# One trunk layer on one core: a new fixed order for preparation and attention heads, q copies on ScalarE, head 2's query weights made inside head 0

## The chip, the cores and the metric

One of the eight cores of a Trainium2 chip runs the whole program. The metric is device time in microseconds (us) of one execution. The engines of a core are TensorE (PE in the profile, PEld for its weight loads), VectorE (DVE), ScalarE (ACT), GpSimd (POOL) and SyncE (SP, which here only issues transfers).

## The reference

One layer of a diffusion backbone in fp32, D = 1024, 8 heads, for two streams with shared weights: 512 latent tokens and 128 context tokens, 640 columns in all.

```python
mod = silu(cond) @ w_ada + b_ada          # shift1, scale1, gate1, shift2, scale2, gate2
h = rms_norm(x) * (1 + scale1) + shift1
u, q, k, v, gates = split(h @ w_in)
q, k = rope_2d(q), rope_2d(k)             # latent tokens only
s = q @ k.T / 8                           # two maps per head
a = softmax(s0) - lam * softmax(s1)
o = rms_norm(a @ v); y_b = o @ w_proj_b; y_a = pool(u) @ w_proj_a
x += gate1 * ((sigmoid(gA) * y_a + sigmoid(gB) * y_b) @ w_out)
h = rms_norm(x) * (1 + scale2) + shift2
x += gate2 * ((silu(dwconv3(h @ Wa)) * (h @ Wu)) @ w_ffn_out)
```

Latent queries see 128 cached context keys and their own 512; the context tokens see themselves alone. The context's keys and values are outputs too.

## The kernel before

Every matrix product is done in three passes on two halves of each operand: `x = hi + lo`, where hi is x rounded to the reduced format fp32r, and hi*hi + hi*lo + lo*hi are added in PSUM. So each weight (128 x 1024, one 512 KB transfer) costs a cast for hi (ACT, L126) and a subtraction for lo (DVE or POOL, L127) before TensorE can use it; `wcols` and `wload` do this with the engines they are given.

The program has a boot, the attention, a mixing stage, an output stage and a feed-forward stage. The boot makes the modulation vectors and `hT`, the normalised and modulated tokens, transposed, and projects q and k of head 0 and q of head 1 (`q`, `k`, `w` in its list). The order of its steps is written out by hand in the string `BOOT`; each token is a letter for the step and a number: `n` sum of squares (ACT), `i` normalising (DVE), `x` transpose (PE), `y` copy from PSUM (ACT for tiles 0 to 3, DVE for 4), `d`/`l` high and low part of a modulation weight (ACT/DVE), `a` its matmuls, `r` copy of a row (ACT, L418), `c` its turn to columns (PE), `u` putting it away (DVE), `h`, `m`, `t` high part, full and low part of `hT` (ACT, DVE, DVE; the last `t` on POOL), `s`/`z` high and low part of the first q and k weights (ACT/POOL, L447/L451). Every instruction of the list is pinned, that is, it is issued behind all that was written before it for its engine.

The attention goes head by head, by the nine strings of `PHASES`. `Stm` is one score map (token tile t, map m): four matmuls on a PSUM bank of two (`psS`), a row maximum on DVE (`nm`, L688), an exponential on ACT (L690), and with the second map a reciprocal and a product (L695, L696), a scaling (ACT, L697) and the joining of the two maps (DVE, L698). `T` transposes the joined map of the head before, `P` multiplies it by the values. `p` is one of eight steps of a projection of q or k of a coming head, `b` one of twenty of v, and `x` transposes the head's context keys and the cached keys on a bank that it shares with the scores. In these strings only the matmuls are pinned. What the other engines do is put in order by the framework's scheduler.

After a projection `rope` (L555) turns q or k: ACT copies it from PSUM, DVE shuffles it (L561), POOL multiplies by the cosine (L562), DVE by the sine (L563) and adds (L564). `q_part` (L573) then splits q: for each of two halves ACT copies a high part into one half of the partitions of `qd` (L582), DVE makes the low part `ql` (L583), POOL copies the high part into the other half (L584). `k_split` does the same for k: high part by ACT (L598), low part by DVE (L599). `weights` starts the load of a weight and of the next one in a list when the first is used; by it, the first use of v's first weight (`b` in phase 0) starts the load of head 2's q weight, whose low part POOL makes.

Of the kernel before, what the change touches and what calls it, by code (L numbers as in the profile page):

```python
# [14 lines left out]
ALU = mybir.AluOpType  # L15
# [3 lines left out]
P = 128  # L19
D = 1024  # L20
KD = D // P
# [13 lines left out]
COL_U, COL_Q, COL_K, COL_V, COL_G = 0, 512, 1536, 2560, 3584  # L35
# [32 lines left out]
def trunk_kernel(ctx: ExitStack, tc: tile.TileContext, a: dict, o: list):  # L68
    nc = tc.nc
# [7 lines left out]
    w_ada, w_in = a["w_ada"][0], a["w_in"][0]  # L77
# [33 lines left out]
    def f(ap):  # L111
        return ap.bitcast(F32)
# [18 lines left out]
    def wcols(w, c0, ncol, k0, nk, name, eng=nc.vector, cp=nc.scalar):  # L131
        src = w[k0 * P:(k0 + nk) * P, c0:c0 + ncol].rearrange("(k p) n -> p k n", p=P)
        return wload(src, (nk, ncol), name, eng, cp)
# [19 lines left out]
    dve, act, pool = Pin(nc.vector), Pin(nc.scalar), Pin(nc.gpsimd)  # L153
# [138 lines left out]
    with tc.tile_pool(name="boot", bufs=1, reuse_waits="tile") as boot:  # L292
        chunks = [(which, col, q) for q in range(4) for which, col in (("sh1", 0), ("sc1", D))]
        XT_ACT = (0, 1, 2, 3)
        H_POOL = (7,)
        BOOT = ("n0 i0 n1 x0 i1 n2 x1 y0 i2 n3 x2 n4 i3 a00 y1 i4 y2 x3 a01 y3 d10 x4 d11 l10 r0 s0 l11 c0 a10 z0 u0 "
# [4 lines left out]
        pinned[0] = True  # L301
        vc_ = boot.tile([16, P], F32, tag="vc", name="vc")
        vr = boot.tile([V_END - 16, P], F32, tag="vr", name="vr")
# [159 lines left out]
        P0 = {}  # L463
# [20 lines left out]
    PBUFS = 7  # L484
    MIX = "u0 8g n0 1g n1 2g m0 4g n2 u1 1g n3 1g m1 2g n4 1g n5 1g u2 1g m2 2g n6 1g n7 u3 1g m3 14g"
    PHASES = (
# [9 lines left out]
    G, sig = {}, {}  # L496

    def gate_load(j, i):
# [27 lines left out]
    with tc.tile_pool(name="att", bufs=2, reuse_waits="tile") as att:  # L526
# [25 lines left out]
            nc.vector.tensor_tensor(neglam, lsum[:, 1:2], lsum[:, 0:1], ALU.subtract)  # L552
            nc.vector.tensor_scalar(neglam, neglam, LAM_INIT, None, ALU.subtract)

        def rope(ps, name, scale):  # L555

            sh = att.tile([P, TOK], F32, tag="rsh", name=f"rsh_{name}")[:, :LAT]
            y_ = att.tile([P, TOK], F32, tag="ry", name=f"ry_{name}")
            nc.scalar.activation(two(y_), ps[:, :, :HALF], AF.Copy, scale=scale)
            y = y_[:, :LAT]  # L560
            nc.vector.stream_shuffle(sh, y, SHUF)  # L561
            nc.gpsimd.tensor_tensor(y, y, cos, ALU.mult)  # L562
            nc.vector.tensor_tensor(sh, sh, sin, ALU.mult)  # L563
            nc.vector.tensor_tensor(y, y, sh, ALU.add)  # L564
            return y_

        def q_load(h):
            return wcols(w_in, COL_Q + h * P, P, 0, KD, f"q{h}", nc.gpsimd)

        def k_load(h):  # L570
            return wcols(w_in, COL_K + h * P, P, 0, KD, f"k{h}", nc.gpsimd)
# [1 line left out]
        def q_part(h, ps=None, bank=bankP):  # L573
            if ps is None:
                w = weights("q", h)
                ps = bank(f"psq{h}")
                yield from proj_steps(ps, w, hT)
            y = rope(ps, f"q{h}", 0.125)
            qd = [att.tile([P, TOK], F32R, tag=f"qd{m}", name=f"qd{m}_{h}") for m in range(2)]
            ql = QL[h % 2]  # L580
            for (r, o, t), (_, _, l) in zip(MAPS(qd), MAPS(ql)):
                nc.scalar.copy(t[r], y[r])  # L582
                nc.vector.tensor_tensor(l[r], y[r], f(t[r]), ALU.subtract)  # L583
                nc.gpsimd.tensor_copy(t[o], f(t[r]))  # L584
            Q[h] = qd, ql

        def MAPS(pair):
# [37 lines left out]
        def k_part(h, ps=None):  # L625
            if ps is None:
                w = weights("k", h)
                ps = bankP(f"psk{h}")
                yield from proj_steps(ps, w, hT)
            y = rope(ps, f"k{h}", 1.0)  # L630
            k_split(h, y, slice(P, KEYS))
            Y[h] = y

# [88 lines left out]
        def values(h, i):  # L722

            vh, vl = V[h // 2]
            vc = slice((h % 2) * P, (h % 2 + 1) * P)
            if i == 0:
                PO[h] = bank1(f"po{h}")
            po, k0 = PO[h], 2 * i
            pt, th, tl = TT[h, k0]
            for i in range(2):  # L730
                kt = k0 + i
                if kt < 5:
                    mm3(po, vh[kt][:, vc], vl[kt][:, vc], th[:, i, :], tl[:, i, :], kt == 0, kt == 4)
            if k0 < 4:
                return
            pp = pt[:, 1, 256:384]
            mm3(pp, vh[5][:, vc], vl[5][:, vc], th[:, 1, :P], tl[:, 1, :P], True, True)
            nc.scalar.copy(oraw[:, h, :LAT], po)
            nc.scalar.copy(oraw[:, h, LAT:], pp)
            sq = att.tile([P, TOK], F32, tag="rsh", name=f"sq{h}")  # L740
            nc.gpsimd.tensor_tensor(sq, oraw[:, h, :], oraw[:, h, :], ALU.mult)
            sh = att.tile([P, TOK], F32R, tag="th", name=f"sqh{h}")
            sl = att.tile([P, TOK], F32R, tag="tl", name=f"sql{h}")
            nc.scalar.copy(sh, sq)
            nc.vector.tensor_tensor(sl, sq, f(sh), ALU.subtract)
            SQ[h] = sh, sl
# [44 lines left out]
        W = {}  # L791

        def weights(kind, i):

            n = need.index((kind, i))
            for st in need[n:n + 2]:
                if st not in W:
                    W[st] = loads[st[0]](st[1])
            return W[kind, i]

# [14 lines left out]
        def step(h, op):  # L815
            kind, i = op[0], int(op[1:] or 0) if op[0] in "STPm" else 0
            if op[-1] == "g":
                gate_steps(int(op[:-1]))
            elif op[-1] in queue:
                project(op[-1], int(op[:-1] or 1))  # L820
            elif kind == "S":
                attend(h, i // 10, i % 10)
            elif kind == "T":
                turned(h - 1, i)
            elif kind == "P":
                values(h - 1, i)
            elif kind == "m":
                u_pool(i)
            else:
                between(NH + 1 if kind == "z" else h)  # L830
# [175 lines left out]
    h2 = mg  # L1006
# [576 lines left out]
```

## Time and profile before

| | us |
|---|---|
| median of 3 runs | 1090.98 (1090.66 to 1093.48) |
| the profiled execution | 1091.43 |
| its span, first to last instruction | 1089.6 |

The profile is one execution on the hardware. A time of a row is counted from the span's start. Busy time of TensorE is that of its matmuls, whose ends are modelled. The granted clock is given as a share of full speed. In its page TensorE is busy for 1038.0 us of the span, DVE for 851.6, ACT for 543.5 and POOL for 320.8.

### The profile page before, as it was taken

To read this page: it belongs to the slowest core of one execution; us is meant where nothing else is said; L and a number is where in the kernel's file an instruction comes from. 1 tells how busy PE (TensorE), PEld (TensorE's weight loads), DVE (VectorE), ACT (ScalarE), POOL (GpSimd) and SP (SyncE) were. 2 spreads that over 40 slices of the span, in tenths; PEclk is the share of its full clock that TensorE was granted. 3 is DMA by queue.
4 is the path that set the end of the run, shared out by engine and by line. 5 is a ranking of instruction groups with operands and counts; after the bars stand their busy time and mean duration, and the time that the engine had idled before them with its cause. 6 is when DMAs were issued, how large, how long until landed. Compare 5 with 4: busy or idle time off the path is not lost.

```text
span 1089.6 us, 16713 instructions
## 1 busy us (share of the span) xinstructions
PE 1038.0 (95%) x6559; PEld 967.0 (89%) x6559; DVE 851.6 (78%) x1193; ACT 543.5 (50%) x906; POOL 320.8 (29%) x256
## 2 busy tenths in 40 slices
PE   6979999999999999999999999899989999999997
PEld 4778899999999999999998899898779998899986
DVE  5978978988887577776773579998889984699947
ACT  8646666666765552222242465554345542255524
POOL 4544224323222630000000005443374420444202
PEclk9999999999999999999999999999999999999999
DMA  9831212202112135545554022223442322323312
GB/s 312 247 88 51 62 32 69 59 25 71 38 43 59 41 96 157 165 140 159 154 190 141 1 78 59 83 92 93 127 128 82 94 68 68 97 78 94 119 38 97
DMA packets 128481, 106.10 MB, mean 97 GB/s; under 512 B 4174, under 2 KB 110206, under 8 KB 128403
## 3 DMA queue, kind: packets, MB, share of 16 engines
q1 hardware_dynamic: 126450, 101.93, 30.8%
q0 software_dynamic: 1232, 1.80, 0.8%
q8 instruction: 51, 0.84, 0.3%
q10 hardware_dynamic: 720, 1.31, 0.3%
q14 instruction: 28, 0.22, 0.1%
HBM read 101.36 MB, written 3.67 MB: 96 GB/s over the span
## 4 chain that ended last, share of the span: by engine, by line
PE 54%; DVE 28%; ACT 8%; issue 7%; POOL 1%; DMA 1%; SPq 0%; ACTq 0%; DVEq 0%; POOLq 0%
PE ps_g L157 10%; DVE cv L150 7%; PE psyb L157 5%; PE psk L157 3%; PE psu L157 3%; PE psya L157 3%; DVE wlo_f L150 3%; PE s L157 2%; PE acc L157 2%; PE po L157 2%; DVE nm L688 2%; PE psv L157 2%; PE psq L157 2%; ACT cv L150 1%; PE pat L160 1%
## 5 line engine op out<-in xcount | busy, mean ns | idle before, releaser
L150 POOL TENSOR_TENSOR s<-raw_fu 128x512 f32<-128x512 f32 x20 | 33.3, 1666 | 309.1 <-DVE spare L150 155.7
L150 DVE SCALAR_TENSOR_TENSOR cv<-av,vcol,cv 128x511 f32<-128x511 f32 (+1 forms) x80 | 88.8, 1130 | 12.1 <-ACT cv L150 10.8
L157 PE MATMUL ps_g<-hT,whi_g 128*128 128x320 f32 x512 | 96.7, 311 | 0.0
L157 PEld LDWEIGHTS ps_g<-hT,whi_g 128*128 128x128 f32 x512 | 80.2, 188 | 2.0 <-issue 1.5
L690 ACT ACTIVATE p<-s,nm 128x640 f32<-128x640 f32 (+1 forms) x80 | 56.7, 709 | 40.0 <-DVE nm L688 39.4
L688 DVE TENSOR_REDUCE nm<-s 128x1 f32<-128x640 f32 (+1 forms) x80 | 56.5, 709 | 12.4 <-PE s L157 11.0
L157 PE MATMUL psv<-whi_v,hT 128*128 128x256 f32 x320 | 66.0, 286 | 0.0
L157 PE MATMUL ps_g<-hT,wlo_g 128*128 128x320 f32 x256 | 58.3, 309 | 0.0
L150 DVE TENSOR_TENSOR wlo_f<-s,whi_f 128x1024 fp32r<-128x1024 f32 x40 | 51.0, 1298 | 4.7 <-ACT whi_f L150 4.6
L157 PE MATMUL s<-ks,qd 128*128 128x320 f32 x144 | 44.2, 318 | 10.7 <-DVE ks L599 7.1
L157 PEld LDWEIGHTS psv<-whi_v,hT 128*128 128x128 f32 x320 | 53.2, 192 | 0.3 <-ACT whi_v L126 0.3
L157 PE MATMUL psyb<-on,whi_pb 128*128 128x320 f32 x256 | 48.0, 309 | 0.0
L150 ACT CAST whi_f<-s 128x1024 fp32r<-128x1024 f32 x40 | 41.8, 1044 | 12.0 <-POOL s L150 11.9
L157 PE MATMUL psv<-wlo_v,hT 128*128 128x256 f32 x160 | 45.5, 284 | 0.9 <-DVE wlo_v L127 0.9
L157 PE MATMUL s<-ks,ql 128*128 128x320 f32 x144 | 42.9, 308 | 0.0
L157 PEld LDWEIGHTS ps_g<-hT,wlo_g 128*128 128x128 f32 x256 | 42.8, 188 | 0.0
L157 PE MATMUL psk<-hT,whi_k 128*128 128x320 f32 x224 | 42.6, 312 | 0.0
L157 PEld LDWEIGHTS psyb<-on,whi_pb 128*128 128x128 f32 x256 | 40.3, 188 | 0.5
L697 ACT ACTIVATE p<-p,z 128x640 f32<-128x640 f32 (+1 forms) x40 | 29.7, 744 | 20.0 <-DVE z L696 19.8
L157 PEld LDWEIGHTS s<-ks,qd 128*128 128x128 f32 x144 | 27.6, 192 | 13.4 <-POOL ry_q L562 6.8
L698 DVE SCALAR_TENSOR_TENSOR p<-p,z,p 128x640 f32<-128x640 f32 (+1 forms) x40 | 35.0, 878 | 5.4 <-ACT p L697 5.1
L150 POOL TENSOR_TENSOR acc_g<-acc_g,part_g 128x512 f32<-128x512 f32 x16 | 27.9, 1743 | 37.7 <-ACT part_g L150 36.8
(985 smaller groups left out, 3409.9 us busy)
## 6 DMA issues: line engine op xcount, KB each, us to landing
raw_fa<-in_w_ffn_in_dram SPq DMA_DIRECT2D x22, 512.0 KB, 3.8
raw_fu<-in_w_ffn_in_dram SPq DMA_DIRECT2D x22, 512.0 KB, 3.8
raw_fo<-in_w_ffn_out_dram SPq DMA_DIRECT2D x20, 512.0 KB, 3.6
raw_g<-in_w_in_dram SPq DMA_DIRECT2D x16, 512.0 KB, 4.9
raw_g<-in_w_ada_dram SPq DMA_DIRECT2D x16, 512.0 KB, 3.7
araw_sh<-in_w_ada_dram SPq DMA_DIRECT2D x8, 512.0 KB, 7.6
araw_sc<-in_w_ada_dram SPq DMA_DIRECT2D x8, 512.0 KB, 8.3
raw_v<-in_w_in_dram SPq DMA_DIRECT2D x8, 512.0 KB, 6.3
```

The lines of the kernel that those rows point to most:

```text
L150: pin(getattr(self.eng, op)(*args, **kw))
L157: pin(nc.tensor.matmul(out, s, m, start=start, stop=stop, skip_group_check=more))
L160: pin(nc.tensor.transpose(out, x, ident))
L688: nc.vector.tensor_reduce(nm[:, i:i + 1], s, AX.XY, ALU.max, negate=True)
L690: nc.scalar.activation(p.rearrange("p (b n) -> p b n", b=s.shape[1]), s, AF.Exp, bias=nm[:, i:i + 1], accum_out=z[:, i:i + 1])
L697: nc.scalar.activation(p, p, AF.Copy, scale=z[:, 1:2])
L698: nc.vector.scalar_tensor_tensor(A[h, t], A[h, t], z[:, 0:1], p, ALU.mult, ALU.add)
```

## The change

Five things are edited. The string `BOOT` has the same 143 steps in another order. Of the nine phase strings all but that of phase 4 have their steps in another order, and that of phase 0 has one new step, `w`. `rope` takes the engine of the cosine multiply, which is now DVE for q of heads 0 and 1 and for k of head 0, and POOL for the rest. The copy of q's high part into the other partitions is on ACT instead of POOL, in all heads. Head 2's query weight is no longer loaded with the first use of v's weight but at `w` in phase 0, behind the step `x`, with the cast on ACT and the low part on DVE, both pinned there.

```diff
-        BOOT = ("n0 i0 n1 x0 i1 n2 x1 y0 i2 n3 x2 n4 i3 a00 y1 i4 y2 x3 a01 y3 d10 x4 d11 l10 r0 s0 l11 c0 a10 z0 u0 "
-                "y4 v d20 a11 r1 l20 c1 d21 u1 a20 h0 l21 d30 m0 a21 h1 t0 l30 k0 r2 s2 q0 m1 d31 z2 a30 t1 d40 c2 "
-                "l31 k1 d41 l40 q1 a31 l41 d50 w0 r3 l50 c3 d51 w1 u2 u3 l51 h2 a50 a40 h3 m2 a51 t2 d60 a41 m3 r5 "
-                "d61 l60 k2 c5 r4 l61 s1 q2 c4 d70 z1 u5 t3 w2 d71 u4 l70 k3 h4 a60 l71 a70 h5 m4 a61 t4 a71 m5 r6 "
-                "c6 k4 r7 c7 u6 t5 q3 u7 h6 w3 k5 h7 m6 q4 t6 w4 m7 k6 t7 q5 w5 q6 w6 k7 q7 w7 ")
+        BOOT = ("n0 n1 i0 x0 i1 n2 x1 i2 y0 n3 x2 i3 n4 a00 y2 i4 x3 a01 y3 d10 x4 y1 d11 l10 r0 s0 l11 c0 z0 a10 u0 "
+                "y4 v d20 a11 r1 l20 d21 c1 d30 u1 a20 h0 l21 m0 a21 h1 l30 t0 k0 s2 r2 d31 m1 a30 t1 d40 z2 c2 k1 "
+                "l31 q0 d41 l40 a31 l41 d50 w0 q1 r3 c3 l50 d51 w1 u2 u3 l51 h2 a50 h3 m2 a51 m3 a40 t2 d60 a41 r5 "
+                "d61 r4 l60 k2 l61 s1 c4 c5 t3 d70 u5 q2 z1 d71 w2 a60 u4 k3 l70 h4 l71 a70 h5 m4 a61 r6 t4 a71 m5 c6 "
+                "q3 k4 r7 u6 c7 t5 u7 h6 w3 h7 m6 t6 w4 k5 m7 q4 q5 t7 k6 w5 w6 q6 k7 q7 w7")
...
     PHASES = (
-        "3b p 4b 2p 2b S00 S01 2b p S10 2p x p S11 p b S20 2b S21 b S30 3b S31 S40 2b",
-        "3p S00 p S01 2p x 2p T0 S10 4p S11 T1 p P0 p S20 2p S21 P1 T2 2p P2 p S30 p S31 2p S40 2p",
-        "b S00 b S01 b 2p x b T0 b 3p S10 p P0 S11 T1 b p 2b S20 P1 p T2 S21 4b P2 b S30 3b S31 2b S40 2b",
-        "3p S00 S01 2p x T0 3p S10 P0 S11 2p T1 S20 3p T2 p S21 2p P1 P2 S30 3p S31 2p S40 3p",
+        "4b 2p b p 4b S00 b S01 x w b p S10 3p S11 b S20 p 2b S21 3b S30 2b S31 S40 b",
+        "2p S00 2p S01 2p x 2p T0 S10 4p S11 T1 P0 2p S20 2p S21 T2 P1 2p P2 p S30 p S31 2p S40 2p",
+        "b S00 b S01 b 2p b T0 b p x 3p S10 b P0 S11 T1 p 2b S20 P1 p T2 S21 5b S30 P2 3b S31 b S40 3b",
+        "S00 3p S01 2p x T0 3p S10 P0 S11 2p T1 S20 4p T2 p S21 p P1 P2 S30 4p S31 2p S40 2p",
-        "2p S00 S01 2p x T0 4p S10 P0 S11 p T1 2p S20 3p T2 2p S21 P1 P2 p S30 S31 5p S40 2p",
-        "S00 b S01 b p b x 3p S10 p b T0 2p S11 b T1 b S20 p 2b P0 P1 S21 T2 5b S30 b P2 2b S31 b S40 3b",
-        "2p S00 S01 3p x T0 2p S10 p P0 T1 p S11 2p P1 S20 p S21 2p T2 2p S30 P2 p S31 S40 2p",
-        "3p x p m0 m1 p T0 T1 m2 5p T2 P0 p P1 P2 2p 1g m3 3g z 1g")
+        "2p S00 S01 3p x T0 3p S10 P0 S11 p T1 2p S20 3p T2 2p S21 P1 P2 p S30 S31 5p S40 2p",
+        "S00 b S01 b p b x 4p b S10 T0 2p S11 T1 2b S20 p 2b P0 P1 S21 T2 5b S30 b P2 2b S31 b S40 3b",
+        "p S00 p S01 3p x T0 2p S10 p P0 T1 p S11 2p P1 S20 p S21 2p T2 2p S30 P2 p S31 S40 2p",
+        "2p x 2p m0 m1 p T0 T1 m2 5p P0 T2 p P1 P2 2p 1g m3 3g z 1g")
...
-        def rope(ps, name, scale):
+        def rope(ps, name, scale, eng=nc.gpsimd):
-            nc.gpsimd.tensor_tensor(y, y, cos, ALU.mult)
+            eng.tensor_tensor(y, y, cos, ALU.mult)
-        def q_load(h):
-            return wcols(w_in, COL_Q + h * P, P, 0, KD, f"q{h}", nc.gpsimd)
+        def q_load(h, *eng):
+            return wcols(w_in, COL_Q + h * P, P, 0, KD, f"q{h}", *(eng or (nc.gpsimd,)))
...
-            y = rope(ps, f"q{h}", 0.125)
+            y = rope(ps, f"q{h}", 0.125, nc.gpsimd if h > 1 else nc.vector)
             for (r, o, t), (_, _, l) in zip(MAPS(qd), MAPS(ql)):
-                nc.gpsimd.tensor_copy(t[o], f(t[r]))
+                nc.scalar.copy(t[o], f(t[r]))
...
-            y = rope(ps, f"k{h}", 1.0)
+            y = rope(ps, f"k{h}", 1.0, nc.gpsimd if h > 0 else nc.vector)
...
             for st in need[n:n + 2]:
-                if st not in W:
+                if st not in W and (st, kind) != (("q", 2), "v"):
                     W[st] = loads[st[0]](st[1])
...
                 values(h - 1, i)
+            elif kind == "w":
+                W["q", 2] = q_load(2, dve, act)

```

## Rows read from the trace of the kernel before

**Rows 1.** TensorE's waits from 60 to 108.4 us: total, times, longest.

```profile
PE s L157 <- DVE ks L599: 6.6, 1, 6.6
...
PE s L157 <- ACT p L690: 1.7, 2, 1.3
```

**Rows 2.** Windows: stretch, length; busy PE, PEld, DVE, ACT, POOL; clock; DMA share, GB/s.

```profile
60.00:345.00 285.00, 268.27 (x1868) 257.66 (x1867) 238.56 (x384) 187.24 (x364) 88.43 (x67) 0.99 0.18 52
...
75.30:81.90 6.60, 0.03 (x1) 0.01 (x1) 6.34 (x8) 3.53 (x6) 4.20 (x3) 0.74 0.03 8
...
81.90:108.40 26.50, 24.24 (x163) 23.29 (x163) 22.74 (x35) 17.74 (x37) 11.09 (x8) 0.94 0.17 53
```

**Rows 3.** Windows of one microsecond: the first and last of four.

```profile
82.00:83.00 1.00, 1.00 (x4) 1.00 (x5) 0.97 (x2) 0.00 (x0) 0.00 (x0) 0.50 0.00 0
...
85.00:86.00 1.00, 1.00 (x10) 1.00 (x9) 0.85 (x2) 0.82 (x4) 0.00 (x0) 0.87 0.00 0
```

**Rows 4.** Order of time of DVE and POOL, 64 to 83 us: start, duration, instruction.

```profile
66.24 1.23 DVE L127 TENSOR_TENSOR wlo_v<-raw_v,whi_v 128x1024 fp32r<-128x1024 f32 x1 [1.26 <-ACT whi_v L126]
...
67.39 0.74 DVE L561 STREAM_SHUFFLE rsh_q<-ry_q 128x512 f32<-128x512 f32 x1
...
69.45 2.86 POOL L127 TENSOR_TENSOR wlo_q<-raw_q,whi_q 128x1024 fp32r<-128x1024 f32 x1
...
69.97 2.89 DVE L563 TENSOR_TENSOR rsh_k<-rsh_k,sin 128x512 f32<-128x512 f32 x1
...
72.78 1.78 DVE L564 TENSOR_TENSOR ry_q<-ry_q,rsh_q 128x512 f32<-128x512 f32 x1
...
79.28 0.69 DVE L563 TENSOR_TENSOR rsh_q<-rsh_q,sin 128x512 f32<-128x512 f32 x1
...
80.00 2.62 DVE L599 TENSOR_TENSOR ks<-ry_k,ks 64x640 fp32r<-64x640 f32 x2
```

**Rows 5.** Instructions on the tile qd: count, shortest, median and longest ns.

```profile
L582 ACT CAST qd<-ry_q x16: 712/724/731, 74.6 to 288.8; 64x640 fp32r<-64x640 f32 x16
...
L583 DVE TENSOR_TENSOR ql<-ry_q,qd x16: 812/1107/1270, 75.4 to 290.9; 64x640 fp32r<-64x640 f32 x16
```

**Rows 6.** The chain that ended last, 60 to 112 us: start, duration, what.

```profile
92.71 0.87 PE psk L157 x6
...
93.58 0.71 PE psv L157 x6
...
94.30 0.60 PE s L157 x4
```

**Rows 7.** Order of time of POOL, DVE and PE at head 0's end.

```profile
102.67 2.42 POOL L127 TENSOR_TENSOR wlo_q<-raw_q,whi_q 128x1024 fp32r<-128x1024 f32 x1 [3.99 <-ACT whi_q L126]
...
103.25 3.37 DVE L599 TENSOR_TENSOR ks<-ry_k,ks 64x640 fp32r<-64x640 f32 x2
...
106.34 0.31 PE L157 MATMUL s<-ks,qd 128*128 128x320 f32 x1
```

**Rows 8.** TensorE's waits from 108 to 345 us.

```profile
PE mx L160 <- ACT p L690: 3.3, 3, 1.4
...
PE pat L160 <- ACT p L690: 1.5, 1, 1.5
...
PE s L157 <- DVE tl L714: 1.3, 1, 1.3
```

**Rows 9.** Order of time of ACT and PE in the boot.

```profile
13.69 1.91 ACT L382 COPY xT<-pt 128x1024 f32<-128x1024 f32 x2
...
16.29 1.01 ACT L382 COPY xT<-pt 128x1024 f32<-128x1024 f32 x1 [0.69 <-PE pt L160]
...
19.09 0.36 ACT L418 COPY rows_sh<-ps_sh 4x256 f32<-4x256 f32 x1
...
19.50 0.60 PE L157 MATMUL ps_sh<-sel,rows_sh 5*128 5x2 f32 x4 [0.41 <-ACT rows_sh L418]
...
20.86 1.05 ACT L398 CAST xn_sh<-araw_sh 128x1024 fp32r<-128x1024 f32 x1 [0.45 <-DMA araw_sh<-in_w_ada_dram]
```

## The prediction

> **What bounds the kernel now.** I read the page first, then a table of windows over the whole span, then TensorE's waits, and last the order of time where those waits are longest. From 345 us on TensorE is nearly always busy and the change touches nothing there. What can move lies ahead of it. Between 60 and 345 us TensorE is busy for 268.27 of 285 us [rows 2], so 16.7 us are idle. The list of waits says where. One wait alone is 6.6 us: the first score matmul of head 0, held by the DVE operation that makes the low part of head 0's keys [rows 1]. The windows show the same stretch: from 75.3 to 81.9 us TensorE has 0.03 us of work [rows 2]. A second loss hangs on it. After that idle stretch the granted clock stands at 0.50, the lower of its two levels (1.2 instead of 2.4 GHz), for the first scores too, and returns at about 85.9 us [rows 3]; the four windows from 82 to 86 us show 0.50, 0.50, 0.50 and 0.87, which is 1.63 us of work lost. So the hole at head 0 costs 6.6 + 1.6 = 8.2 us. The waits of the later heads are smaller: their three largest groups make 6.1 us together [rows 8]. The largest of them, 3.3 us, is at the step `x`, whose PSUM bank is freed by an exponential on ScalarE.
>
> Why is the hole there? The time order [rows 4] is to be read as two engines in each other's way. DVE shuffles q and k of head 0 from 67.39 us on. Then POOL takes up the low part of head 2's query weights for 2.86 us, and the DVE multiply beside it (128x512, by the sine) takes 2.89 us, where the same operation with POOL idle takes 0.69 us. POOL's cosine multiply of k comes only after that weight, so k is late as well. In the end the low part of k starts at 80.00 us and takes 2.62 us for two.
>
> **The change, part by part.** (1) *The preparation of head 0.* It removes from POOL three cosine multiplies (q0, k0, q1), the weight q2 and the two q copies, and puts the cosines and the weight on DVE, the copies on ScalarE. Without POOL beside them I take 0.69 us for each DVE multiply or add and 0.72 us from start to start [rows 4]. Two shuffles from 67.39 us at a pitch of 0.64 end DVE's first part at 68.67 us. Six operations at 0.72 us (cosine, sine, add for q and for k) end at 73.0 us. ScalarE has four copies for q, the added two priced like the two there now, 0.724 us each [rows 5], so 2.9 us from q's add (70.8) to 73.75 us; then one copy for k to 74.5 us and one DVE subtraction of 0.81 us [rows 5], which gives 75.4 us; the first score needs only this first half of the keys. If the two low parts of q (2 x 0.81) go ahead of k's three operations, it is 76.3 us. The matmuls ahead of the first score are as many as before: 9 `b` and 3 `p` in the old phase string, 9 `b` and 3 `p` in the new one, so the cover still ends at 75.3 us. The wait of 6.6 us becomes 0.1 to 1.0 us; I take 0.6, so 6.0 us saved. With so short a wait the clock has no such idle stretch to fall after, and the 1.6 us come back too: 7.6 us. If POOL's work were gone but DVE did the whole rope of q1 first (a shuffle, three operations and two subtractions, 4.5 us), only about 1.5 us would be saved.
>
> The Trainium skill, page SBUF — State Buffer, section Who interferes with whom, says that a DVE instruction with two SBUF inputs contends with a GpSimd instruction that reads SBUF, and that whoever began first holds the shared port for its whole instruction. The 2.89 us beside 0.69 us [rows 4] agree. By that rule the gain isn't complete, since POOL keeps k1's cosine and the low parts of two weights in head 0, and it speaks for the second case below; the sum would then be the 1088.2 worked out there.
>
> (2) *What DVE has to give back in head 0.* On DVE the change adds 3 x 0.69 us and one weight's low part, 1.23 us like the one of v [rows 4], together 3.3 us. It takes away stretched time: 2.2 us at the sine, 1.1 us at q's add (1.78 against 0.69), 1.0 us at k's low part [rows 4], and in q0 and q1 four times the 0.295 us between median and shortest of that subtraction, 1.2 us [rows 5]: 5.5 us. So DVE ends 2.2 us ahead, no more, if it is what sets the pace up to the first score of head 1, which waits for the low part of k1 that runs 3.37 us for two beside POOL's 2.42 us [rows 7]. Now that score starts at 106.34 us; by DVE alone it would be at 104.1. By TensorE alone: one `p` is 0.87 us, one `b` 0.71 us, one score of four matmuls 0.60 us [rows 6]; from the first score of head 0 at 76 us it has 11 `b`, 7 `p`, eight scores, the shorter last one and the transposes (0.9 us for both, an estimate from the 0.60), 7.8 + 6.1 + 4.8 + 0.9 = 19.6 us, and with 1.5 us of waits for exponentials (1.7 us now [rows 1]) this ends at 97.1 us. One `p` that was ahead of that score before now comes after it, so 0.88 us more work is still to do. The stretch therefore gains between 106.34 - 0.88 - 104.1 = 1.3 us and 106.34 - 0.88 - 97.1 = 8.4 us. DVE is busy 22.74 of the 26.5 us here [rows 2], so it is near the limit but has 3.8 us of gaps to fill, and its low-ranking work (the joining of the two maps) may run after the score. I take two thirds of the added 3.3 us as given back, 2.2 us: 7.6 - 2.2 = 5.4 us gained.
>
> (3) *The later heads.* Between the first score and `x` phase 1 now has 4 `p` for 3, phase 3 has 5 for 2, phase 5 has 3 for 2. At 0.87 us each [rows 6] that is 0.9, 2.6 and 0.9 us more cover, against 3.3 us of waits at three `x` [rows 8]. POOL's q copies no longer stretch q's low part, 0.6 us of DVE a head. Against this ScalarE gets 2 x 0.724 us a head [rows 5], and phase 3 starts its scores without the three `p` ahead. Bounds: 4.6 us saved (the 3.3 us at `x` and the 1.3 us at a score; the 1.5 us at a transpose lie in phase 4, whose string stays), or up to 10.1 us lost (seven heads with 1.45 us each). I take 2.0 us saved: most of the `x` waits go, some of it returns at ScalarE.
>
> (4) *The boot order.* ScalarE's copy of token tile 1 goes behind tile 3 and the first weight cast. ScalarE waits 0.69 us for tile 3 as it is, and without a copy to fill that time the second cast and the copy of the modulation row at 19.09 us come 0.95 us later, half of the 1.91 us that two copies take; TensorE waits for just that row now [rows 9]. Later a DVE low part of h goes behind a weight's, 1.2 us. Against it, ScalarE waits 0.45 us for a transfer soon after [rows 9] and can take that up. Bounds: 1 us gained to 2.2 us lost; I take 0.5 us lost. Head 2's query weight is needed only at the start of phase 1, with 10 `b` and 5 `p` after its step `w` (11.4 us), and this is what hides its cast of 1.05 us (a cast of that size in [rows 9]); its DVE part is priced in (2).
>
> Sum: -5.4 - 2.0 + 0.5 = -6.9 us. The profiled execution took 1091.43 us (span 1089.6), so 1084.5; the median of the three runs lies 0.45 us lower, which gives 1084.0 us.
>
> **The rivals.**
> *DVE sets head 0's pace.* The lower end of (2): only 1.3 us gained there, then -2.0 and +0.5: -2.8 us, 1088.2 us. For it: DVE's 22.74 of 26.5 us. Against: the hole itself comes from an order of work, not from DVE's amount.
> *The later heads lose nearly all waits.* 4.6 us instead of 2.0 in (3), the rest as forecast: 1081.4 us. For it: the extra `p` stand just where the waits are. Against: each head has its own wait, and phases 2 and 4 keep theirs.
> *The wait stays.* DVE's order puts q1's rope or v's low part ahead of k0, 4.5 to 5 us, and the first score comes at 80 to 82 us: 1.0 us saved at the middle, the clock's loss stays, the boot takes its 0.5, nothing else moves, so 1090.5 us. For it: these operations aren't pinned in the text and their order on DVE is the scheduler's. Against: it has placed q0 and k0 first so far [rows 4].
> *Slower: ScalarE's copies delay exponentials.* Two copies stand in ScalarE's queue ahead of an exponential that frees a score bank; if seven heads wait 1.45 us longer for this, 10.1 - 5.4 + 0.5 = +5.2 us, 1096 us. It turns the sign from four heads on (4 x 1.45 = 5.8 us against 4.9). For it: `x` waits for ScalarE already [rows 8]. Against: in 60 to 345 us ScalarE is busy 187.24 of 285 us [rows 2]; the copies bring it to 70%. The Trainium skill, TensorE: Matmul & The Clock Gate, section on the array's architectural detail, calls ScalarE's queue strictly first in, first out; by that rule an exponential can't pass a copy and this case stands at 1096. The trace, where `x` waits for exponentials while ScalarE has idle time elsewhere, doesn't contradict it.
>
> **How the numbers follow.** Chances: forecast 0.50 (its own range 1081.8 to 1086.6), DVE's pace 0.18, later heads 0.17, wait stays 0.08, slower 0.07. The range leaves out the last two and the tail below 1079.5: 1079.5 to 1089.0. About 0.3%, 3.3 us, is what a measurement here tells from no change: the line is 1087.7. Faster are forecast, later heads and 0.07 of DVE's pace, 0.74; within the bound 0.11 and the 0.08, 0.19; slower 0.07.
>
> **What would show it.** Right: no idle stretch over 1 us before head 0's first score and that score at about 76 us, a granted clock of 1.00 throughout 70 to 90 us, the sine multiplies of q0 and k0 at 0.7 us each, and head 1's first score at about 100 us. (2) is wrong if that score waits for k1's low part by more than 4 us. (3) shows in TensorE's waits at `x`: 3.3 us now, under 1.5 then. (4) shows in TensorE's wait for the modulation row, 0.41 us now [rows 9]. The whole is wrong if the first score still waits for DVE, or if ScalarE's exponentials become what most scores wait for.

## The result, and the profile after

The changed kernel takes 1081.38 us in the median (1080.8 to 1083.6, six runs), the kernel before on the same chip 1093.37 us (1090.66 to 1095.63, six runs). The ratio is 0.9896, with a 95% interval of 0.9877 to 0.9915. The profiled executions have spans of 1079.8 and 1089.6 us, 9.8 us apart. (The medians are 12 us apart: the kernel before was profiled in one of its shorter executions.)

First TensorE's waits after the change, as total, times and longest: the first two lines are of 60 to 100 us, the third of 100 to 345 us.

```profile
PE s L157 <- ACT p L690: 2.7, 3, 1.4
...
PE s L157 <- ACT qd L584: 0.3, 1, 0.3
...
PE pat L160 <- ACT p L690: 3.3, 2, 1.8
```

The wait of 6.6 us for the keys' low part in [rows 1] is gone; in its place the first score waits 0.3 us for a copy on ScalarE (L584). No wait at `x` is left of the 3.3 us in [rows 8], but 3.3 us stand at transposes (`pat`), where there were 1.5.

Windows after (stretch, length; busy PE, PEld, DVE, ACT, POOL; clock; DMA share, GB/s):

```profile
60.00:345.00 285.00, 276.09 (x1934) 265.65 (x1933) 239.24 (x410) 202.78 (x387) 69.48 (x55) 1.00 0.18 54
70.00:80.00 10.00, 9.41 (x69) 8.74 (x68) 9.11 (x15) 6.89 (x13) 0.20 (x1) 1.00 0.11 32
80.00:90.00 10.00, 9.68 (x69) 9.22 (x68) 8.91 (x17) 9.20 (x16) 1.08 (x2) 1.00 0.25 74
```

In the same 285 us TensorE is busy 276.09 us where it was 268.27 [rows 2], and the granted clock is 1.00 from 70 to 90 us, where it had fallen to 0.50 [rows 3]. ScalarE is at 202.78 of 285 us, 71%.

The order of time after, from the preparation of head 0 to head 1's first score (start, duration, instruction, idle time ahead of it):

```profile
69.09 0.67 DVE L562 TENSOR_TENSOR ry_q<-ry_q,cos 128x512 f32<-128x512 f32 x1
69.68 0.68 DVE L563 TENSOR_TENSOR rsh_q<-rsh_q,sin 128x512 f32<-128x512 f32 x1
...
71.49 0.68 DVE L564 TENSOR_TENSOR ry_q<-ry_q,rsh_q 128x512 f32<-128x512 f32 x1
...
73.01 1.67 DVE L583 TENSOR_TENSOR ql<-ry_q,qd 64x640 fp32r<-64x640 f32 x2 [0.24 <-ACT qd L582]
...
73.75 1.48 ACT L598 CAST ks<-ry_k 64x640 fp32r<-64x640 f32 x2
...
74.71 1.67 DVE L599 TENSOR_TENSOR ks<-ry_k,ks 64x640 fp32r<-64x640 f32 x2
75.25 1.48 ACT L584 CAST qd<-qd 64x640 fp32r<-64x640 f32 x2
76.03 0.41 PE L157 MATMUL s<-ks,qd 128*128 128x320 f32 x1 [0.27 <-ACT qd L584]
...
83.27 1.22 DVE L150 TENSOR_TENSOR wlo_q<-raw_q,whi_q 128x1024 fp32r<-128x1024 f32 x1
...
89.28 2.40 POOL L127 TENSOR_TENSOR wlo_k<-raw_k,whi_k 128x1024 fp32r<-128x1024 f32 x1 [8.92 <-ACT whi_k L126]
...
94.26 2.35 POOL L127 TENSOR_TENSOR wlo_q<-raw_q,whi_q 128x1024 fp32r<-128x1024 f32 x1 [0.88 <-ACT whi_q L126]
...
94.78 0.67 DVE L662 TENSOR_TENSOR v<-psv,v 128x512 fp32r<-128x512 f32 x1
...
95.82 0.33 PE L157 MATMUL s<-ks,qd 128*128 128x128 f32 x1 [1.43 <-ACT p L690]
...
98.98 1.67 DVE L599 TENSOR_TENSOR ks<-ry_k,ks 64x640 fp32r<-64x640 f32 x2
99.95 0.39 PE L157 MATMUL s<-ks,qd 128*128 128x320 f32 x1 [0.93 <-ACT p L690]
```

The cosine and sine multiplies of q0 take 0.67 and 0.68 us on DVE, one behind the other, where a sine beside POOL had taken 2.89 us [rows 4]. Both halves of k0's low part take 1.67 us (2.62 before [rows 4]), those of k1's 1.67 us too (3.37 before [rows 7]). Head 2's query weight has its low part at 83.27 us in 1.22 us, six microseconds ahead of POOL's next weight. Head 1's first score is at 99.95 us instead of 106.34 [rows 7].

To see where the 9.8 us came from, four moments of each trace are enough. A is the first matmul of v on the low part of the second half of its weight, just behind the end of the boot's work on TensorE. B is the first score of head 0, C its last (the 128x128 form), D the first matmul of the mixing stage (`psu`). The column D-A leaves out the boot. D is read to 0.1 us, and what is worked out from it is good to about that. One thing in it is not equal work: the new string of phase 0 has 19 `b` ahead of C, the old one 18, so with a new string B to C holds 0.71 us more [rows 6] and C to D as much less.

| kernel | A | B-A | C-B | D-C | D-A | span |
|---|---|---|---|---|---|---|
| before | 67.52 | 14.40 | 19.79 | 212.2 | 246.4 | 1089.6 |
| changed | 67.94 | 8.09 | 19.79 | 209.1 | 237.0 | 1079.8 |
| e1_q2_back | 69.44 | 10.24 | 22.01 | 209.7 | 242.0 | 1087.8 |
| e2_cos_pool | 69.64 | 8.90 | 21.25 | 210.1 | 240.3 | 1086.7 |
| e3_copy_pool | 68.40 | 8.55 | 25.15 | 210.4 | 244.1 | 1088.7 |
| e4_old_boot | 69.03 | 8.08 | 19.81 | 209.1 | 237.0 | 1080.4 |
| e5_old_later | 67.84 | 8.09 | 19.81 | 214.1 | 242.0 | 1086.9 |
| e6_ops_only | 68.90 | 8.09 | 23.41 | 213.7 | 245.2 | 1090.2 |
| e7_order_only | 67.56 | 14.42 | 22.21 | 210.8 | 247.4 | 1091.2 |
| a0_again | 69.82 | 8.08 | 19.83 | 209.1 | 237.0 | 1081.6 |
| v1_low_dve | 68.75 | 8.08 | 20.01 | 207.4 | 235.5 | 1080.1 |
| v2_k1cos_dve | 67.94 | 8.07 | 19.37 | 210.4 | 237.9 | 1081.3 |
| v3_strings | 69.72 | 8.09 | 19.80 | 210.2 | 238.1 | 1082.1 |
| n1_fill | 69.25 | 14.46 | 18.87 | 216.4 | 249.8 | 1095.8 |

Before against changed: +0.4 to A, -6.3 to B, 0.0 to C, -3.1 to D. From D to the end it is 775.7 and 774.9 us, -0.8. Together -9.8.

### The profile page after: what moved, and what is told of

It is laid out like the page before. It is cut to its first block, busy times and chain, and to the rows that moved or that the text cites. A ratio compares the mean times of both kernels' runs of the same rounds, so it can differ in the third digit from the quotient of the medians.

```text
span 1079.8 us, 16691 instructions
## 1 busy us (share of the span) xinstructions
PE 1036.0 (96%) x6559; PEld 966.0 (89%) x6559; DVE 844.0 (78%) x1197; ACT 554.3 (51%) x922; POOL 294.2 (27%) x236
## 3 DMA queue, kind: packets, MB, share of 16 engines
q10 hardware_dynamic: 720, 1.31, 0.3%
## 4 chain that ended last, share of the span: by engine, by line
PE 53%; DVE 25%; ACT 9%; issue 8%; POOL 2%; DMA 1%; SPq 1%; ACTq 0%; DVEq 0%; POOLq 0%
PE ps_g L157 10%; DVE cv L150 7%; PE psyb L157 5%; PE psk L157 3%; DVE wlo_f L150 3%; PE psu L157 3%; PE psya L157 3%; PE s L157 2%; PE psv L157 2%; PE acc L157 2%; PE po L157 2%; PE psq L157 2%; DVE nm L688 1%; ACT cv L150 1%; DVE acc_g L150 1%
## 5 line engine op out<-in xcount | busy, mean ns | idle before, releaser
L126 ACT CAST whi_g<-raw_g 128x1024 fp32r<-128x1024 f32 x16 | 16.8, 1049 | 43.1 <-PE ps_g L157 23.7
L157 PE MATMUL pb<-mg,whi_f 128*128 128x320 f32 x176 | 38.7, 307 | 0.0
```

The costliest lines, as they stand in the source:

```text
L126: cp.copy(hi[:, :n], rv)
L157: pin(nc.tensor.matmul(out, s, m, start=start, stop=stop, skip_group_check=more))
```

## The experiments

Ratios are against the kernel before on the same chip, with 95% intervals. The first four each undo one part of the change.

**e1_q2_back**: head 2's query weight is again started by v's first weight, with POOL for its low part.

```diff
-                if st not in W and (st, kind) != (("q", 2), "v"):
+                if st not in W:
-        "4b 2p b p 4b S00 b S01 x w b p S10 3p S11 b S20 ...
+        "4b 2p b p 4b S00 b S01 x b p S10 3p S11 b S20 ...
```

> The changed kernel with head 2's query weight back where it was: loaded with the first use of v's weight, its low part on POOL. Theory (POOL and DVE block each other when both read SBUF, so POOL's 2.9 us stretch a DVE operation of head 0's keys by up to 2.2 us): head 0's first score waits 1.5 to 2.5 us instead of 0.3 and the span is 0.5 to 2.5 us over the changed kernel's 1079.8 us. Rival (the harm before was POOL's queue alone, with k's cosine behind the weight; the cosine is on DVE now): that score stays at 76.0 us within 0.3, and the span stays or falls by up to 1 us, since DVE is rid of 1.2 us in head 0.

Measured: 0.9951 [0.9932, 0.9969], 1088.48 us. D-A is 242.0 against 237.0, so the weight's place and its engine together are worth 5.0 us; no run moves one of the two alone. Order of time, and a window of two microseconds behind the first score:

```profile
70.46 2.41 POOL L127 TENSOR_TENSOR wlo_q<-raw_q,whi_q 128x1024 fp32r<-128x1024 f32 x1 [8.26 <-ACT whi_q L126]
70.59 2.83 DVE L562 TENSOR_TENSOR ry_q<-ry_q,cos 128x512 f32<-128x512 f32 x1
...
79.68 0.41 PE L157 MATMUL s<-ks,qd 128*128 128x320 f32 x1 [2.43 <-ACT qd L584]
```

```profile
81.00:83.00 2.00, 2.00 (x10) 1.96 (x9) 1.85 (x4) 1.34 (x3) 0.00 (x0) 0.50 0.00 0
```

The collision of [rows 4] is back, with the multiply by the cosine in the sine's place: 2.83 us beside POOL's 2.41. The first score then waits 2.43 us, as forecast, and the clock falls to 0.50 behind it. The cost is double the upper end of the forecast: 2.1 us are lost ahead of the first score, 2.2 more up to C and 0.7 behind it. The Trainium skill, SBUF — State Buffer, section Who interferes with whom, has DVE instructions with two SBUF inputs wait while GpSimd holds their common port; these rows agree.

**e2_cos_pool**: the three cosine multiplies back on POOL.

```diff
-            y = rope(ps, f"q{h}", 0.125, nc.gpsimd if h > 1 else nc.vector)
+            y = rope(ps, f"q{h}", 0.125, nc.gpsimd)
-            y = rope(ps, f"k{h}", 1.0, nc.gpsimd if h > 0 else nc.vector)
+            y = rope(ps, f"k{h}", 1.0, nc.gpsimd)
```

> The changed kernel with the cosine multiplies of q0, k0 and q1 back on POOL. Theory (an operation on POOL holds up DVE's one beside it, so nothing is gained by two engines): POOL needs about 1.3 us where DVE needs 0.7, the sines beside it stretch, head 0's first score comes 1 to 2 us later than 76.0, span +0.5 to +2. Rival (they overlap, so DVE is spared 0.7 us for each): the first score comes 0 to 1 us earlier, span -1 to 0.

Measured: 0.9936 [0.9916, 0.9955], 1086.34 us; D-A 240.3, so 3.3 us for this part. The order of time on the two engines:

```profile
70.32 1.31 POOL L562 TENSOR_TENSOR ry_q<-ry_q,cos 128x512 f32<-128x512 f32 x1 [7.91 <-DVE rsh_q L561]
70.80 1.38 DVE L563 TENSOR_TENSOR rsh_q<-rsh_q,sin 128x512 f32<-128x512 f32 x1
71.57 1.76 POOL L562 TENSOR_TENSOR ry_k<-ry_k,cos 128x512 f32<-128x512 f32 x1
72.10 1.78 DVE L563 TENSOR_TENSOR rsh_k<-rsh_k,sin 128x512 f32<-128x512 f32 x1
```

A cosine on POOL beside a sine on DVE ends 1.86 us after the first began (70.80 + 1.38 - 70.32) for q, 2.31 us for k. One behind the other on DVE they take 1.27 us (69.09 to 69.68 + 0.68). Here two engines side by side are slower than one. Of the 3.3 us only some 0.8 lie ahead of the first score, less than the 1 to 2 us forecast; 1.5 lie between B and C, where `x` waits 1.6 us for an exponential, and 1.1 behind C. So the whole cost is above the forecast.

**e3_copy_pool**: the second copies of q's high part back on POOL, in all heads.

```diff
-                nc.scalar.copy(t[o], f(t[r]))
+                nc.gpsimd.tensor_copy(t[o], f(t[r]))
```

> The changed kernel with the copies of q's high part back on POOL in all heads. Theory (the copies stretch DVE's low part beside them, 0.3 us each): span +1 to +3 us. Rival (ScalarE is what the scores wait for in the changed kernel: 6.6 us of TensorE's waits between 60 and 345 us name its exponentials, and the 16 copies take 11.6 us of its time): these waits shrink by a half or more and the span falls by 1 to 3 us.

Measured: 0.9981 [0.9968, 0.9994], 1091.09 us; D-A 244.1, 7.1 us for this part, more than twice the upper end of the forecast, and 5.4 of them between B and C. The order of time at head 0's end, and a window behind it:

```profile
96.69 2.34 POOL L127 TENSOR_TENSOR wlo_q<-raw_q,whi_q 128x1024 fp32r<-128x1024 f32 x1 [1.73 <-ACT whi_q L126]
96.83 2.74 DVE L564 TENSOR_TENSOR ry_k<-ry_k,rsh_k 128x512 f32<-128x512 f32 x1
...
102.10 0.47 PE L157 MATMUL s<-ks,qd 128*128 128x128 f32 x1 [5.27 <-ACT p L690]
```

```profile
103.00:105.00 2.00, 2.00 (x11) 2.00 (x11) 1.61 (x5) 1.35 (x5) 0.00 (x0) 0.50 0.00 0
```

The low part of a later weight now falls on k1's addition, which takes 2.74 us; the last score of head 0 waits 5.27 us and the clock is at 0.50 behind it. That a relief of ScalarE would make the kernel faster is refuted. How much of the 7.1 us is the copies' own time on POOL and how much is that they push this weight onto the addition isn't told apart.

**e4_old_boot**: the old string `BOOT`, all else as changed.

```diff
-        BOOT = ("n0 n1 i0 x0 i1 n2 x1 i2 y0 ...
+        BOOT = ("n0 i0 n1 x0 i1 n2 x1 y0 i2 ...
```

> The changed kernel with the old order of the boot. Theory (the new boot order costs 0.4 us, as the start of v's second matmuls shows, 67.94 after 67.52 us): span 0.2 to 0.6 us shorter. Rival (the new boot order is part of the gain, because it puts other work beside the first projections): span longer by 0.5 us or more.

Measured: 0.9898 [0.988, 0.9916], 1082.53 us, with D-A of 237.0 as in the changed kernel. The boot's order is worth nothing that can be measured.

The next three split the change into orders and operations.

**e5_old_later**: the old strings of phases 1 to 8; phase 0, boot and engines as changed.

```diff
-        "2p S00 2p S01 2p x 2p T0 S10 4p S11 T1 P0 ...
-        "b S00 b S01 b 2p b T0 b p x 3p S10 ...
...
+        "3p S00 p S01 2p x 2p T0 S10 4p S11 T1 p P0 ...
+        "b S00 b S01 b 2p x b T0 b 3p S10 ...
...
```

> The changed kernel with the old strings from phase 1 on; boot, phase 0 and the engines stay as changed. From the start of v's second matmuls to the first matmul of the pooling projection the kernel before takes 246.4 us, the changed one 237.0. Theory (of these 9.4 us, 3.5 us fall after head 0's end, and the new strings bring them by putting cover before x): 239 to 241 us, the waits at x back at 2 to 3.3 us. Rival (they come from POOL's relief, the strings bring nothing): 236.5 to 238 us.

Measured: 0.9958 [0.9944, 0.9973], 1088.95 us; D-A 242.0, so the later strings are worth 5.0 us with the new engines, 1.0 us more than the upper end of the forecast. An order of time around TensorE's largest single wait from 110 to 345 us, three windows of this phase 2, and the cast of the same phase in the kernel before:

```profile
140.07 1.09 PE L160 MATMUL pat<-ident,p 128*128 128x128 f32 x8
...
142.78 1.48 ACT L584 CAST qd<-qd 64x640 fp32r<-64x640 f32 x2
144.16 1.00 ACT L713 CAST th<-pat 128x1024 fp32r<-128x1024 f32 x1
...
146.48 0.41 PE L157 MATMUL s<-ks,qd 128*128 128x320 f32 x1 [1.96 <-DVE tl L714]
```

```profile
146.00:148.00 2.00, 1.52 (x9) 1.52 (x10) 1.83 (x4) 0.00 (x0) 0.00 (x0) 0.87 0.00 0
148.00:150.00 2.00, 2.00 (x7) 1.71 (x7) 0.20 (x1) 1.29 (x3) 0.00 (x0) 0.50 0.00 0
150.00:152.00 2.00, 2.00 (x11) 1.76 (x11) 0.65 (x2) 0.00 (x0) 0.00 (x0) 0.77 0.13 38
```

```profile
148.64 1.02 ACT L713 CAST th<-pat 128x1024 fp32r<-128x1024 f32 x1
```

This is the place where ScalarE's new copies cost something. The cast `th` of the transposed map (L713) stands behind the two copies of 142.78 us in ScalarE's queue and begins 4.09 us after T0's transposes (140.07 to 144.16); in the kernel before, with the copies on POOL, it was 2.34 us (146.30 to 148.64). `tl` follows on DVE, and the score waits 1.96 us, where the same wait was 1.27 us, the 1.3 of [rows 8]. Then the clock falls: 0.87, 0.50 and 0.77 in three windows of 2 us are 1.7 us lost (0.26 + 1.00 + 0.46). With the 0.7 us of the wait that is 2.4 us. D-C of this kernel is 2.6 us above that of before at equal work (214.1 + 0.71 against 212.2). That the copies are the cause is read from these rows; no run takes them off ScalarE in this order. The new string of phase 2 puts `x` and a `p` between T0 and S10, and the wait is gone. The Trainium skill, TensorE: Matmul & The Clock Gate, section on the array's architectural detail, has ScalarE's queue strictly in order; the row of `th` agrees.

**e6_ops_only**: the old boot and phase strings with the new engines. Since head 2's weight needs a place, `w` is put behind `x`, as in the new string. The edit is shown against the changed kernel.

```diff
-        "4b 2p b p 4b S00 b S01 x w b p S10 3p S11 ...
+        "3b p 4b 2p 2b S00 S01 2b p S10 2p x w p S11 ...
...
```

> The kernel before with the new engines alone: cosines of q0, k0, q1 on DVE, q copies on ScalarE, head 2's query weight at a step w behind x in the old phase 0; boot and phase strings old. Theory (the hole at head 0 is closed by the engines): first score at 76 us, the stretch of 246.4 us falls to 239 to 241.5 us. Rival (the old phase 0 doesn't fit the new engines, so the wait comes back at the next scores): 243 us or more.

Measured: 1.0003 [0.9989, 1.0018], 1092.81 us. The operations alone bring nothing; the rival of the expectation (243 us or more) holds. The hole ahead of B is closed as in the changed kernel (8.09 us), but C-B is 23.41 us. TensorE's waits from 60 to 110 us, the order of time inside head 0, and a window behind C:

```profile
PE s L157 <- ACT p L690: 4.9, 5, 1.9
```

```profile
92.59 2.39 POOL L127 TENSOR_TENSOR wlo_k<-raw_k,whi_k 128x1024 fp32r<-128x1024 f32 x1 [1.13 <-ACT whi_k L126]
93.29 2.78 DVE L150 TENSOR_TENSOR wlo_q<-raw_q,whi_q 128x1024 fp32r<-128x1024 f32 x1
...
99.13 0.41 PE L157 MATMUL s<-ks,qd 128*128 128x320 f32 x1 [1.90 <-ACT p L690]
```

```profile
102.00:104.00 2.00, 2.00 (x12) 2.00 (x11) 2.00 (x4) 1.05 (x3) 1.73 (x1) 0.56 0.00 0
```

Scores wait five times for exponentials, 4.9 us together, and the clock falls behind the last. In this string `x` stands three scores in, so `w` comes ten microseconds later than in the changed kernel, beside POOL's next weight, and its low part takes DVE 2.78 us instead of 1.22. Against e5, which has the new phase 0, D-A is 3.2 us longer (245.2 to 242.0). How much of it is the place of `w`, which was my choice, and how much the order of scores and `p` isn't told apart.

**e7_order_only**: the kernel before with the new strings (without `w`) and its old engines. The edit is shown against the kernel before.

```diff
-        BOOT = ("n0 i0 n1 x0 i1 n2 x1 y0 i2 ...
-        "3b p 4b 2p 2b S00 S01 2b p S10 ...
+        BOOT = ("n0 n1 i0 x0 i1 n2 x1 i2 y0 ...
+        "4b 2p b p 4b S00 b S01 x b p S10 ...
...
```

> The kernel before with the new boot and phase strings alone, no engine moved and no w. Theory: the wait at head 0's first score stays above 5 us and the clock falls after it; only the later heads gain: 243 to 246 us for the stretch that takes 246.4. Rival (the order of the text is what counts): 240 us or less.

Measured: 1.0002 [0.9991, 1.0013], 1094.14 us. The first line is the wait ahead of B, unchanged from [rows 1]; the second shows that head 0 then waits for exponentials too.

```profile
PE s L157 <- DVE ks L599: 6.6, 1, 6.6
PE s L157 <- ACT p L690: 3.3, 2, 3.1
```

D-A makes it a table of four: before 246.4, operations alone 245.2, orders alone 247.4, both 237.0. The orders alone are 1.0 us longer, where the theory had them gain. For the same reason the prices of e1 to e5 are no shares of the gain: 5.0, 3.3, 7.1, 0.0 and 5.0 add up to 20.4 us, and the whole change brings 9.4.

The last five look for the limits of the account.

**a0_again**: the changed kernel once more, beside the variants v1, v3 and n1, with no edit.

> The changed kernel once more, beside the others of this call on one chip: 1081 to 1083 us, stretch from v's second matmuls to the pooling projection 237.0 us.

Measured: 0.9896 [0.9878, 0.9914], 1082.33 us. Its stages repeat to 0.04 us, but A comes 1.9 us later. The windows of 30 to 60 us of the changed kernel's two executions, first and again:

```profile
30.00:60.00 30.00, 29.10 (x209) 24.85 (x208) 27.85 (x40) 19.13 (x30) 13.04 (x13) 0.97 0.83 221
```

```profile
30.00:60.00 30.00, 29.11 (x191) 24.51 (x190) 26.58 (x36) 18.62 (x28) 12.30 (x12) 0.89 0.79 214
```

The same list of instructions was granted 0.97 of the clock once and 0.89 the other time.

**v1_low_dve**: the low parts of the q and k weights on DVE, not POOL.

```diff
-            return wcols(w_in, COL_Q + h * P, P, 0, KD, f"q{h}", *(eng or (nc.gpsimd,)))
+            return wcols(w_in, COL_Q + h * P, P, 0, KD, f"q{h}", *eng)
-            return wcols(w_in, COL_K + h * P, P, 0, KD, f"k{h}", nc.gpsimd)
+            return wcols(w_in, COL_K + h * P, P, 0, KD, f"k{h}")
```

> The changed kernel with the low parts of all q and k weights of heads 2 to 7 on DVE instead of POOL: 1.2 us each on DVE instead of 2.4 us on POOL, 12 of them or so. Theory (a POOL operation that reads SBUF holds up DVE's next one for about as long as DVE would need for the work itself): the stretch of 237.0 us becomes 235 to 238. Rival (POOL's work is mostly hidden, DVE's isn't): 239 us or more.

Measured: 0.9878 [0.9858, 0.9898], 1081.04 us: the shortest of all, yet its interval overlaps that of a0_again. In the traces D-A is 1.5 us shorter. Its wait at transposes from 110 to 345 us, the last score of head 0, and a window behind that:

```profile
PE pat L160 <- ACT p L690: 0.3, 1, 0.3
```

```profile
96.84 0.33 PE L157 MATMUL s<-ks,qd 128*128 128x128 f32 x1 [1.63 <-ACT p L690]
```

```profile
98.00:100.00 2.00, 2.00 (x10) 2.00 (x9) 1.94 (x5) 1.17 (x4) 0.38 (x1) 0.50 0.56 167
```

The 3.3 us at transposes shrink to 0.3. The other two lines show what is lost again at head 0's end: a wait of 1.63 us with the clock at 0.50 behind it.

**v2_k1cos_dve**: k1's cosine on DVE as well.

```diff
-            y = rope(ps, f"k{h}", 1.0, nc.gpsimd if h > 0 else nc.vector)
+            y = rope(ps, f"k{h}", 1.0, nc.gpsimd if h > 1 else nc.vector)
```

> The changed kernel with the cosine multiply of k1 on DVE as well. Theory (the remaining waits at head 0's end, 1.4 us at the last score and 0.9 us at head 1's first, come from DVE held up by POOL; POOL's 1.7 us there stretch a join of two maps from 0.9 to 1.9 us): these waits fall by 0.5 to 1.5 us and the stretch of 237.0 us becomes 235.5 to 236.7. Rival (DVE is the limit by its own amount of work, and 0.7 us more makes it later): 237.0 to 238.5 us.

Measured: 0.9912 [0.9896, 0.9928], 1084.01 us. The theory fell: head 0 ends 0.4 us sooner, but head 1's first score waits 1.82 us and D-A is 0.9 us longer.

**v3_strings**: phases 3 and 4 with two steps ahead of T0.

```diff
-        "S00 3p S01 2p x T0 3p S10 P0 S11 ...
+        "S00 3p S01 2p x 2p T0 p S10 P0 S11 ...
-        "b S00 3b S01 x 2p T0 2p b S10 b p P0 ...
+        "b S00 3b S01 x 2p 2b T0 2p S10 p P0 ...
```

> The changed kernel with more cover ahead of two transposes of head joins: in phase 3 two p go ahead of T0, in phase 4 two b. They wait 1.8 and 1.5 us now. Theory (such a wait is a matter of the order of text alone): both fall under 0.3 us, nothing takes their place, the stretch of 237.0 us becomes 233.7 to 235 and the time falls by 2 to 3.3 us. Rival (the scores behind wait instead, since exponentials on ScalarE come when they come): 236 to 238 us.

Measured: 0.9919 [0.9903, 0.9936], 1085.27 us; D-A +1.1 us. The waits at T0 are gone, and a score behind them waits in their place, 1.8 us for DVE:

```profile
PE s L157 <- DVE ssq L623: 2.1, 2, 1.8
```

**n1_fill**: the kernel before with 40 needless matmuls in the bank of the first score, ahead of it, which fill the idle stretch.

```diff
             ps = bankS(f"s{name}{m}")
+            if (h, t, m) == (0, 0, 0):
+                for i in range(40):
+                    mm(ps[:, i % 2, :HALF], hT[0][:, 0, :P], hT[0][:, 0, :HALF], True, True)
```

> The kernel before with 40 needless matmuls (5.9 us of work by the shortest pitch) on the first score's PSUM bank, which the real scores overwrite; they lie in the 6.6 us in which TensorE has nothing to do. Nothing else changes, the output is the same. Theory (the 1.6 us that the lower clock costs are lost on top of the wait): granted clock 1.00 from 75 to 90 us, the stretch of 246.4 us becomes 244.5 to 245. Rival (behind the hole DVE sets the pace, so the clock costs nothing): 246 to 246.8 us.

Measured: 1.0046 [1.0032, 1.0061], 1098.44 us. A window, and the row of a later score:

```profile
75.00:90.00 15.00, 12.79 (x89) 12.07 (x88) 13.07 (x15) 6.54 (x10) 7.00 (x6) 1.00 0.12 37
```

```profile
113.45 0.60 PE L157 MATMUL s<-ks,qd 128*128 128x320 f32 x1 [4.62 <-ACT p L693]
```

With the stretch filled the clock stays at 1.00 from 75 to 90 us, and C comes 0.9 us sooner after A (14.46 + 18.87 against 14.40 + 19.79). But the edit also changed the order in which the other engines work, and a wait of 4.62 us appeared at 113.45 us. D-A is 249.8 us, above both the theory and its rival. So the run shows that the fall of the clock hung on the idle stretch and that up to C 0.9 us of the 1.6 came back; it shows nothing about the end of the kernel.

## Why the prediction was right, point by point

The forecast was -6.9 us. By the two traces the change is -9.8 us: head 0 brought 0.5 us more than forecast, the later heads 1.5, the boot 0.1, and 0.8 came behind D. That the time itself lies inside the stated range is in part luck. The kernel before took 1093.37 us in the median beside the changed one, 1090.98 us in the three runs that the forecast started from; on that scale the ratio of 0.9896 makes 1079.6 us, at the very edge of 1079.5 to 1089.0.

**(1) The hole at head 0** was right in place and size. The first score came at 76.03 us (forecast: about 76) after a wait of 0.27 us (forecast: 0.1 to 1.0), the DVE multiplies took 0.67 and 0.68 us, and the clock stayed at 1.00. e1 and e2 show that part of the hole opens again with either the weight or the cosines back on POOL, and e6 that the operations close it with the old strings too. The path to that time was another one. DVE did all four multiplies ahead of both additions, so q's addition began at 71.49 us and not at about 70; ScalarE took k's two copies (73.75 us) ahead of q's second pair; and what came last was the fifth ScalarE copy, not DVE's subtraction for k. These differences happened to cancel. One row was misread as well: POOL wasn't idle beside the sine of 79.28 us in [rows 4], since it began a cosine multiply of 1.70 us at 79.39. The 0.69 us hold all the same, as the 0.68 us of the changed kernel with POOL idle show.

**(2) What head 0 gives back** was right in size. Head 1's first score came at 99.95 us, for about 100. Taking out the 0.88 us of work moved behind it and the boot's 0.4, the gain there is 106.34 - 0.88 - 99.95 + 0.42 = 5.9 us against 5.4. But the step that gave it was incomplete. It let DVE alone give back time and counted TensorE's steps up to head 1 without asking in which order they stand. e6 has the same operations and the old order, and gives 3.6 of the 6.3 us back between B and C (23.41 - 19.79) and 1.5 behind C. With the new phase 0 and old strings behind it (e5) B to C stays at 19.81 us. So what stands where in phase 0, `w` and the steps between the scores, is what lets the gain stay. The 1.6 us of the clock did come back: the granted clock from B to C was 0.92 before and is 1.00 after, over 19.79 us both times. One `b` more (0.71 us) and waits of 2.0 us instead of 1.7 use 1.0 us of it up; where the other 0.6 went isn't found.

**(3) The later heads** is the term that was mis-sized: -2.0 us forecast, -3.5 measured from head 1's first score to D (207.5 - 204.9 + 0.88). TensorE's idle time there falls from 7.45 to 4.74 us, which is 2.7 of the 3.5; the other 0.8 us are shorter busy time at equal work, and no cause was found for them. The forecast was right that `p` ahead of `x` covers the waits: those of phases 1, 3 and 5 are gone. In phase 3 the wait went on to the next step that needs the same exponential, T0, with 1.76 us. What it overlooked is the score of phase 2: `x` moved behind T0 there, and the wait of 1.3 us for `tl` vanished. The likeliest case's own range was missed by 0.4 us for this (1081.38 for 1081.8 at its lower end), and the time is that of the rival in which the later heads lose nearly all waits. That isn't quite what happened, since two waits at transposes remain. Another 0.8 us came behind D. Nothing that the change edits lies there, and from the first matmul on the tile `psyb` to the end the kernels of this study take between 688.8 and 691.6 us (690.2 before, 689.4 changed), so these 0.8 us have no cause that can be named. The whole-run ratios of e1, e2, e3 and e5 put their prices 1 to 2 us above those by D-A, and in these four traces D to the end is 776.2 to 777.1 us, 1.3 to 2.2 us longer than in the changed kernel; that too has no cause that can be named.

**(4) The boot** came out at +0.4 us for +0.5, and the agreement is chance. The column A scatters from 67.5 to 69.3 us over the four kernels with the old order (before, e4, e6, n1) and from 67.6 to 69.8 over the ten with the new one. TensorE's wait for the modulation row did grow from 0.41 [rows 9] to 1.31 us, as the step said, but it is smaller than that scatter.

**The rivals.** *DVE sets head 0's pace* fell: k1's low part is at 98.98 us and TensorE waits 0.93 us there, not 4. *The wait stays* fell with the first score at 76.03 us. The slower rival was right in its mechanism and wrong in its place. The copies delay the cast `th` in phase 2, not the exponentials at `x`: with the old strings and the copies on ScalarE (e5) these waits are 2.3 us, no more than the 3.3 in [rows 8]. The price was 2.4 us once, and the new strings take it out.

## What to carry to other kernels

When operations move between engines and the order was written for the old engines, measure both halves together: here each alone gave 1.000 and both gave 0.990. Look for a DVE operation that runs several times its usual duration beside GpSimd; in e2 handing the cosines to that second engine made the pair of multiplies slower, not faster. And a wait that a new order removes at one step is to be looked for at the next steps behind it: `x` to T0 here, and T0 to a score in v3.

## What the hardware showed that was not expected

A short wait can cost as much again in clock, but its length alone doesn't tell. In e5 the wait of 1.96 us was followed by 1.7 us of clock loss and in v1 one of 1.63 us by a clock of 0.50, while in the changed kernel one of 1.76 us left the clock at 1.00:

```profile
173.99 1.09 PE L160 MATMUL pat<-ident,p 128*128 128x128 f32 x8 [1.76 <-ACT p L690]
```

```profile
174.00:176.00 2.00, 2.00 (x16) 2.00 (x17) 1.01 (x3) 1.58 (x4) 0.30 (x1) 1.00 0.53 159
176.00:178.00 2.00, 1.92 (x13) 1.65 (x12) 1.91 (x4) 1.27 (x3) 0.25 (x1) 1.00 0.10 33
```

And not every DVE operation is held by POOL: beside POOL's weight of 94.26 us the subtraction with an input in PSUM takes 0.67 us (94.78), while the 128x1 product behind it, with both inputs in SBUF, takes 1.25 us until POOL is done:

```profile
95.38 1.25 DVE L696 TENSOR_TENSOR z<-z,neglam 128x1 f32<-128x1 f32 x1
```
